# Sixteen of 22 pairs of column blocks of the upward feed-forward product as seven products of halves, on one Trainium2 core

## The chip, the core and the metric

The kernel runs on one core of a Trainium2 chip. A core has five engines that run side by side, each through its own queue in order: TensorE (PE) multiplies, VectorE (DVE) and ScalarE (ACT) work elementwise, GpSimd (POOL) does small things, and SyncE (SP) issues the transfers (DMA). PE writes into PSUM, eight banks of 128 x 512 f32; everything else lies in SBUF. The metric is the device time of one execution in microseconds; less is better.

## The reference

A trunk of two layers over 512 tokens of width 1024. Each layer has two feed-forward halves (FFN), a mixer of three head groups and a cross-attention. The change touches the FFN alone:

```python
def swiglu_ffn(x, w_up, w_down):
    gate, up = jnp.split(x @ w_up, 2, axis=-1)
    return (jax.nn.silu(gate) * up) @ w_down
...
    for i in range(DEPTH):
        g = norm_g[i]
        ff = swiglu_ffn(rms_norm(h, g[FFN1_PRE]), ffn_w_up[i, 0], ffn_w_down[i, 0])
        h = h + 0.5 * rms_norm(ff, g[FFN1_POST])
```

`w_up` is 1024 x 5632, `w_down` 2816 x 1024. The trunk has four FFNs. Everything is f32.

## The kernel before

**Products.** An f32 product is made of three matmuls of fp32r parts: every operand is split into hi (a rounded copy, made by ACT) and lo (the rest, a subtraction on DVE), and `mm3` (L243) issues hi x hi, hi x lo and lo x hi. `split` (L1317) is the pair of ACT and DVE operations.

**Upward.** The columns of `w_up` go in 44 blocks of 128, in pairs f = 0 to 21: one gate block, one up block. A block is one unit of weights, 1024 x 128, in SBUF as 128 x 1024: SP loads it into one of four raw buffers (`wraw`), `feed` (L436) splits it into `whi` and `wlo`, and `chans` (L637) multiplies it with the normalized, transposed input x (`xhi`, `xlo`, 1024 x 512 tokens) into one bank of PSUM (`ch`): 8 pieces of 128 rows x 3 matmuls, 512 columns each. The first four blocks of an FFN are made in two halves of 256 columns, because x comes token tile by token tile. `silu` (L853) takes silu of the gate bank (`sg`, ACT), multiplies it with the up bank (`hh`, DVE) and splits the result (`hid`, ACT and DVE).

**Downward.** `down` (L661) takes the 22 blocks of `hid` as the stationary operand and `w_down` as the moving one, 512 columns, for two token tiles of 128 at a time: two passes over 22 units of weights. The norm of the result, the update of h and the next x follow (`post`, `pre`).

**Order.** The program is written by generators ("streams": `feed`, `chans`, `silu`, `down` and so on). A planner in the kernel (`run`, L319) has a table of priorities (PRIO) and a rough clock for each engine, and writes down at each step the operation that could start first. What it writes is the order of each engine's queue; on the chip an engine takes its queue in order and waits on semaphores. In the first FFN three further streams run: `setup` with the rope tables, and `memory` (L869), which normalizes, transposes and splits the memory tokens (`mt`, `mn`, `mhi`, `mlo`).

Of the kernel before, what the change touches and what calls it, by code (L numbers as in the profile page):

```python
# [17 lines left out]
P = 128  # L18
# [37 lines left out]
def twice(order):  # L56
# [11 lines left out]
TAIL = 2, 3  # L68
WARM = 14
# [9 lines left out]
        "xhead": (30.98, 0.1), "square": (31.03, 0), "load": (32.65, 4), "none": (32.7, 0.5), "chans": (34.9, 0),  # L79
# [101 lines left out]
class Trunk:  # L181
# [34 lines left out]
    def raw(self, w, k0, nk, *cols):  # L216

        if len(cols) == 2 and isinstance(cols[0], int):
            cols = (cols,)
        n = sum(c[1] for c in cols)  # L220
# [38 lines left out]
class Weave:  # L259
# [3 lines left out]
    def __init__(self, trunk):  # L263
# [5 lines left out]
            "cur": CUR, "b": 8 - CUR, "w": 3, "raw": 4, "xn": 1, "y": 1, "sg": 1, "hh": 2, "jk": 1, "xq": 2, "xp": 2, "xpT": 2}.items()}  # L269
# [3 lines left out]
        self.u, self.raws = {}, {}  # L273
        self.made = self.used = 0
# [161 lines left out]
    def feed(self):  # L436

        k = self.k
        for i in range(len(self.todo)):
            yield ("r", i)  # L440
            raw = self.raws.pop(i)
            nk, n = raw.shape[1:]
            if i - NJ in self.first[1:]:

                yield ("x", self.first.index(i - NJ), NT - 1)
            o = APART if i in self.narrow else 0
# [3 lines left out]
            if i in self.extra:  # L450
                yield ("open", self.extra[i])
                if self.extra[i] == "x":
                    j = 2 * (len(self.todo) - 1 - i)
                    hi, lo = (flat(x[:, j:j + 2]) for x in (k.xhi, k.xlo))
# [5 lines left out]
            else:  # L460
                yield {"w": 1}
                hi, lo = (k.wp.tile([P, 1024 + 64], F32R, name=q, tag=q, bufs=3)[:, o:o + 1024] for q in ("whi", "wlo"))
# [5 lines left out]
            self.count(1, 0)  # L468

# [5 lines left out]
    def spent(self, i):  # L475
        del self.u[i]
        if i not in self.extra:
            self.free(w=1)
# [79 lines left out]
    def junk(self):  # L558
        mixer = self.phases[self.phase][1] == "mixer"
        key = "t2" if mixer else "jk"  # L560
        yield {key: 1}
        return key, self.t2("jk", [P, S]) if mixer else self.pool.tile([P, S], F32, name="jk", tag="jk")
# [74 lines left out]
    def chans(self, n, nj, sink):  # L637
# [15 lines left out]
        for i in range(nj, n):  # L653
            u = yield from self.unit(self.n(i))
# [6 lines left out]
    def down(self, x, i0, order, c, ready):  # L661
# [5 lines left out]
        for half in range(2):  # L667
# [11 lines left out]
            for i, q in enumerate(order):  # L679
                if half == 0 or i:  # L680
                    for e in ready(q, half):
                        yield e
# [8 lines left out]
                if half or i < nk - 1:  # L691
                    self.spent(self.n(n))
                    n += 1
            for t in ts:
                for f in range(2 if tail else 0):
                    cols = slice(f * S, (f + 1) * S)
                    for i, q, u, m in tail:
                        yield "T"
                        k.mm3x(ps[t][f:f + 1], x(q, t), [w[:, :, cols] for w in u], 0, i == 0, i == nk - 1)
                        if t == ts[1] and f:  # L700
                            self.spent(self.n(m))
                    if not f:
# [29 lines left out]
    def all(self):  # L732
# [5 lines left out]
        self.todo, self.first, self.extra, self.narrow = [], [], {}, set()  # L738
        self.mixers = [i for i, p in enumerate(self.phases) if p[1] == "mixer"]
        for i, p in enumerate(self.phases):  # L740
            self.first.append(len(self.todo))
            self.todo += self.units(*p)
            self.extra[self.first[i] + 3] = i
# [24 lines left out]
    def begin(self):  # L768
# [18 lines left out]
        for t in range(NT):  # L787
            xn = self.pool.tile([P, D], F32, name=f"xn{t}", tag=f"hid{NF - 11 - t}") if t else None
# [28 lines left out]
    def ffn(self, l, g):  # L817
        k = self.k
        wup = k.a["ffn_w_up"][l, g // 8]
        self.spare = (f"hid{NF - 8}", f"hid{NF - 9}")  # L820
        self.fired(("open", self.phase))
        self.hid = [None] * NF
# [7 lines left out]
        def sink(i, ps):  # L830
            if i % 2 == 0:
                self.gate = ps
            else:
                self.spawn(self.silu(i // 2, self.gate, ps), i)
            if i == 2 * NF - 1:
# [4 lines left out]
        def ready(q, half):  # L840
            return [] if half else [("hid", NF - 3 if q is None else q)]
# [3 lines left out]
        if self.phase == 0:  # L845
            self.spawn(self.memory())
        self.spawn(self.down(lambda q, t: tuple(self.hid[q][:, x, t * P:(t + 1) * P] for x in range(2)),
                             2 * NF, list(range(NF)), 0.5, ready))
# [4 lines left out]
    def silu(self, f, gate, up):  # L853
        yield {"sg": 1, "hh": 1}
        sg = self.pool.tile([P, S], F32, name="sg", tag="sg", bufs=1)
        hh = self.pool.tile([P, S], F32, name="hh", tag="hh", bufs=2)
# [1269 lines left out]
```

## Time and profile before

| | us |
|---|---|
| three runs: median (lowest, highest) | 2397.37 (2396.85, 2399.01) |
| the profiled execution, its own time | 2396.95 |
| its span, first to last instruction | 2395.2 |
| PE matmul, busy | 2369.4 |
| DVE, busy | 1306.8 |
| ACT, busy | 986.5 |

Busy time of PE is the union of the matmul records, which overlap: it tells that PE hardly ever stands still, not how fast it goes. How fast is read from starts: so many matmuls in so many microseconds. The same holds on a small scale for DVE, where a record is somewhat longer than the distance to the next start. PEld are the weight loads, one ahead of every matmul. The granted clock of PE was 1.00 in all the stretches shown.

### The profile page before, as it was taken

What the parts mean: (1) busy time and instruction counts of PE and PEld (TensorE: products, weight loads), DVE (VectorE), ACT (ScalarE), POOL (GpSimd) and SP (SyncE); (2) the same over time, 40 slices, a digit from 0 to 9 for tenths busy, and PEclk for the clock granted to TensorE, in tenths of its full rate; (3) what the DMA queues carried; (4) which work ended last, traced back from release to release, by engine and by line L of the source; (5) the groups of instructions that cost most, each with busy time, mean ns of one, the idle gap of its engine ahead of it and who ended that gap; (6) DMA issues with size and microseconds to landing.
All of it is one profiled execution on the core that took longest, in us unless ns stands there. A gap on an engine that the chain in (4) does not pass through costs nothing.

```text
span 2395.2 us, 31724 instructions
## 1 busy us (share of the span) xinstructions
PE 2369.4 (99%) x12398; PEld 2001.4 (84%) x12398; DVE 1306.8 (55%) x1926; ACT 986.5 (41%) x1627; POOL 285.7 (12%) x406
## 2 busy tenths in 40 slices
PE   9999999999999999999999999999999999999998
PEld 8888888878889888888888888897888898888887
DVE  5433456887766643334553334578876657333344
ACT  4332344534554542223442223445355545322343
POOL 1000001454200100000000000023442101000000
PEclk9999999999999999999999999999999999999999
DMA  6543455323555343335543334552145644333354
GB/s 177 160 132 97 151 198 145 93 59 118 176 203 176 123 124 97 97 97 177 179 129 97 97 97 172 195 127 84 60 131 180 210 151 140 107 97 97 98 194 157
DMA packets 320972, 323.23 MB, mean 135 GB/s; under 512 B 27075, under 2 KB 262069, under 8 KB 320822
## 3 DMA queue, kind: packets, MB, share of 16 engines
q1 hardware_dynamic: 320822, 321.20, 42.5%
q8 instruction: 97, 1.59, 0.3%
q14 instruction: 53, 0.43, 0.1%
HBM read 301.50 MB, written 19.66 MB: 134 GB/s over the span
## 4 chain that ended last, share of the span: by engine, by line
PE 92%; DVE 4%; ACT 1%; issue 1%; DMA 1%; POOL 1%; SPq 0%; DVEq 0%; POOLq 0%; ACTq 0%
PE ch L139 49%; PE dn L139 26%; PE kv L139 3%; PE tk L139 3%; PE tp L139 1%; PE xs L139 1%; PE xo L139 1%; PE mo L139 1%; PE ms L139 1%; PE iy L139 1%; PE iu L139 1%; PE kk L139 1%; PE mp L139 1%; DVE pair L139 1%; DVE p L139 1%
## 5 line engine op out<-in xcount | busy, mean ns | idle before, releaser
L139 ACT ACTIVATE whi<-wraw 128x1024 fp32r<-128x1024 f32 (+1 forms) x488 | 513.8, 1054 | 979.7 <-PE ch L139 603.2
L139 DVE TENSOR_TENSOR wlo<-wraw,whi 128x1024 fp32r<-128x1024 f32 (+2 forms) x487 | 594.3, 1221 | 579.6 <-ACT whi L139 565.1
L139 PE MATMUL ch<-xhi,whi 128*128 128x512 f32 (+1 forms) x1840 | 674.5, 369 | 0.0
L139 PE MATMUL ch<-xhi,wlo 128*128 128x512 f32 (+1 forms) x1840 | 669.8, 366 | 0.0
L139 PE MATMUL ch<-xlo,whi 128*128 128x512 f32 (+1 forms) x1840 | 657.7, 366 | 0.0
L139 PEld LDWEIGHTS ch<-xhi,wlo 128*128 128x128 f32 x1840 | 345.7, 188 | 57.5
L139 PEld LDWEIGHTS ch<-xhi,whi 128*128 128x128 f32 x1840 | 345.7, 188 | 57.3 <-issue 1.3
L139 PEld LDWEIGHTS ch<-xlo,whi 128*128 128x128 f32 x1840 | 339.1, 188 | 55.4
L139 PE MATMUL dn<-whi,hid 128*128 128x512 f32 x1376 | 373.6, 390 | 0.0
L139 PEld LDWEIGHTS dn<-whi,hid 128*128 128x128 f32 x1376 | 257.4, 188 | 53.0
L139 POOL TENSOR_SCALAR ss<-ss 128x1 f32<-128x1 f32 (+1 forms) x80 | 32.6, 408 | 1656.0 <-ACT jk L139 1512.5
L139 PE MATMUL dn<-wlo,hid 128*128 128x512 f32 x688 | 214.0, 389 | 0.0
L139 DVE TENSOR_TENSOR hh<-sg,ch 128x512 f32<-128x512 f32 x88 | 60.5, 687 | 261.0 <-PE ch L139 257.0
L139 PEld LDWEIGHTS dn<-wlo,hid 128*128 128x128 f32 x688 | 129.1, 188 | 26.9
L139 PE MATMUL tk<-whi,xhi 128*128 128x272 f32 (+2 forms) x192 | 71.7, 374 | 0.0
L139 PE MATMUL tk<-whi,xlo 128*128 128x272 f32 (+2 forms) x192 | 67.4, 351 | 0.0
L139 PE MATMUL tk<-wlo,xhi 128*128 128x272 f32 (+2 forms) x192 | 67.1, 350 | 0.0
L139 POOL TENSOR_TENSOR sr<-tri,hl 128x512 fp32r<-128x512 f32 x48 | 56.7, 1190 | 65.0 <-PE sg L139 39.5
L139 PE MATMUL dn<-whi,xhi 128*128 128x512 f32 x192 | 61.8, 396 | 0.0
L139 DVE TENSOR_TENSOR hid<-hh,hid 128x512 fp32r<-128x512 f32 x88 | 60.2, 684 | 2.4 <-ACT hid L139 2.4
L139 ACT ACTIVATE xhi<-tp 128x512 fp32r<-128x512 f32 x64 | 37.4, 593 | 58.5 <-PE tp L139 58.2
L139 PE MATMUL dn<-wlo,xhi 128*128 128x512 f32 x192 | 60.9, 391 | 0.3 <-DVE wlo L139 0.2
(338 smaller groups left out, 2887.0 us busy)
## 6 DMA issues: line engine op xcount, KB each, us to landing
wraw<-in_ffn_w_up_dram SPq DMA_DIRECT2D x176, 512.0 KB
wraw<-in_ffn_w_down_dram SPq DMA_DIRECT2D x172, 512.0 KB
wraw<-in_w_in_dram SPq DMA_DIRECT2D x32, 512.0 KB
wraw<-in_xa_w_kv_dram SPq DMA_DIRECT2D x32, 512.0 KB
wraw<-in_w_out_dram SPq DMA_DIRECT2D x30, 512.0 KB
wraw<-in_xa_w_o_dram SPq DMA_DIRECT2D x30, 512.0 KB
mch<-memT SPq DMA_DIRECT2D x32, 256.0 KB
xkv<-kvs SPq DMA_DIRECT2D x32, 256.0 KB
```

Of the source, the lines that this page charges most:

```text
L139: return f(*args, **kw)
```

## The change

In each FFN 16 of the 22 pairs (f = 3 to 20 without 9 and 15) are computed otherwise. A pair is a product of 2 x 2 block matrices: the weights by gate/up and by the halves of the 1024 rows (512 each), x by the same halves of rows and by the halves of the tokens (256 each). Eight products of halves give the result; the change takes seven (Strassen's scheme in Winograd's form), of sums of halves.

- `units` and `raw` load a pair as two buffers X and Y of two half-blocks each, every half with a DMA of its own.
- `feed7` makes four pieces: a (X as it is), c and b (sums, in the tile `sums`: three DVE operations of 1024, 512 and 512 elements) and d (half of Y). a, b and c have 1024 elements in a row, d has 512. Each is split as before. There is one more place for weights in an FFN (four, and two halves for d).
- `forms` makes four sums of quarters of x (`form`), once in an FFN, and splits them.
- `products` issues seven products of 4 pieces x 3 matmuls with 256 columns, into four banks; in the order of PE: P1 (a), P6 (c), P2 (d), P7 (c), P5 (b), P3 (b), P4 (a). The banks are called p17, p62, p5 and p34 (the order rows print p).
- `combine` adds them up: a copy on ACT, four operations on DVE (tile `w`), then silu on ACT and the product with it on DVE (`hid`, now kept in f32).
- `hsplit` splits the results of all 22 pairs in the downward product, for each of its two passes the half of the tokens that the pass needs (`hs`); the places for it are those of the sums of x. The split in `silu` goes.
- `memory` starts when the sums of x are there and uses other buffers; a few tiles move; the scratch of the software DMA, which the kernel does not use, is made smaller. The table of priorities gets a line for each of the new streams.

```diff
+SEVEN = [f for f in range(3, NF - 1) if f not in (9, 15)]
...
-        "xhead": (30.98, 0.1), "square": (31.03, 0), "load": (32.65, 4), "none": (32.7, 0.5), "chans": (34.9, 0),
+        "xhead": (30.98, 0.1), "square": (31.03, 0), "load": (32.65, 4), "forms": (33.5, 0), "piece": (31.5, 0.1), "combine": (2.9, 0), "hsplit": (30.5, 0), "split": (33.4, 0), "none": (32.7, 0.5), "chans": (34.9, 0),
...
+    def feed7(self, i):
+        X, Y = (flat(self.raws.pop(j)).rearrange("p (i n) -> p i n", i=2) for j in (i, i + 1))
+        V = self.V
+        yield {"w": 1}
+        a = self.spawn(self.piece((i, "a"), tuple(self.slot((i, "a"), APART)), X))
+        t = self.pool.tile([P, 4, 512], F32, name="sums", tag="sums")
+        yield "V"
+        V.tensor_tensor(out=t[:, 0:2], in0=bc(Y[:, 1], 1, 2), in1=X, op=ALU.add)
+        yield "V"
+        V.tensor_tensor(out=t[:, 2], in0=t[:, 0], in1=X[:, 1], op=ALU.add)
+        yield {"w": 1}
+        c = self.spawn(self.piece((i, "c"), tuple(self.slot((i, "c"), APART)), t[:, 1:3]))
+        yield "V"
+        V.tensor_tensor(out=t[:, 3], in0=t[:, 2], in1=Y[:, 0], op=ALU.add)
+        yield {"w": 1}
+        b = self.spawn(self.piece((i, "b"), tuple(self.slot((i, "b"), APART)), t[:, 0:4:3]))
+        yield {"wh": 1}
+        h = self.halves
+        self.halves = 1 - h
+        d = self.spawn(self.piece((i, "d"), tuple(self.pool.tile([P, 512 + 64], F32R, name=q, tag=f"{q}h{h}")[:, APART:APART + 512] for q in ("whi", "wlo")),
+                                  Y[:, 0:1]))
+        yield a
+        self.free(raw=1)
+        yield d
+        self.free(raw=1)
+        yield c
+        yield b
...
+            if self.n(i) in self.seven:
+                yield from self.products(i)
+            if self.n(i) in self.seven or self.n(i - 1) in self.seven:
+                continue
...
+    def products(self, i):
+        f, i = i // 2, self.n(i)
+        yield ("forms",)
...
+        a = yield from self.unit((i, "a"))
+        yield {"cur": 1}
+        ps = bank("p17")
+        self.spawn(self.combine(f, banks), 2 * f)
+        yield from prod(ps[:, lo], a, 0, x(0, 0))
+        self.fire(("P1", f))
+        c = yield from self.unit((i, "c"))
+        yield {"cur": 1}
+        p2 = bank("p62")
+        yield from prod(p2[:, lo], c, 1, s2)
+        d = yield from self.unit((i, "d"))
+        yield from prod(p2[:, hi], d, 0, x(1, 0))
+        self.fire(("P2", f))
+        self.spent((i, "d"))
+        yield from prod(ps[:, hi], c, 0, s3)
+        self.fire(("P7", f))
+        self.spent((i, "c"))
+        b = yield from self.unit((i, "b"))
+        yield {"cur": 1}
+        yield from prod(bank("p5")[:, lo], b, 0, s1)
+        self.fire(("p5", f))
+        yield {"cur": 1}
+        ps = bank("p34")
+        yield from prod(ps[:, hi], b, 1, x(1, 1))
+        self.spent((i, "b"))
+        yield from prod(ps[:, lo], a, 1, s4)
+        self.fire(("p4", f))
+        self.spent((i, "a"))
...
+    def combine(self, f, banks):
...
+        w = self.pool.tile([P, 6, 256], F32, name="w", tag="w")
+        yield ("P1", f)
+        yield "S"
+        SC.activation(out=w[:, 4], in_=banks["p17"][:, 0:256], func=AF.Copy)
+        yield ("P2", f)
+        yield "V"
+        V.tensor_tensor(out=w[:, 0:6:5], in0=two(banks["p62"]), in1=bc(w[:, 4], 1, 2), op=add)
+        self.drop(banks["p62"])
+        yield ("P7", f)
+        yield "V"
+        V.tensor_tensor(out=w[:, 1], in0=banks["p17"][:, 256:512], in1=w[:, 0], op=add)
+        self.drop(banks["p17"])
+        yield ("p5", f)
+        yield "V"
+        V.tensor_tensor(out=w[:, 0:4:2], in0=bc(banks["p5"][:, 0:256], 1, 2), in1=w[:, 0:2], op=sub)
+        self.drop(banks["p5"])
+        yield ("p4", f)
+        yield "V"
+        V.tensor_tensor(out=w[:, 3:5], in0=two(banks["p34"]), in1=w[:, 0:2], op=add)
+        self.drop(banks["p34"])
+        yield {"sg": 1}
+        sg = self.pool.tile([P, 2, 256], F32, name="sg", tag="sg", bufs=1)
+        yield "S"
+        SC.activation(out=sg, in_=w[:, 4:6], func=AF.Silu)
+        yield "V"
+        V.tensor_tensor(out=two(self.hidden(f)), in0=w[:, 2:4], in1=sg, op=ALU.mult)
+        self.free(sg=1, seven=1)
+        self.swapped.add(f)
+        self.fire(("hid", f))
...
+    def forms(self):
...
+        a11, a12, a21, a22 = f32
+        self.sx = [form(j) for j in range(4)]
+        t11, t21, t = temp(10), temp(9), temp(8)
+        yield from add(t11, *a11)
+        yield from add(t21, *a21)
+        yield from add(t, t11, t21, ALU.subtract)
+        last = [self.spawn(self.split(*self.sx[2], t))]
+        yield from add(t21, t21, a22[0], ALU.subtract)
+        yield from add(t21, t21, a22[1], ALU.subtract)
+        last.append(self.spawn(self.split(*self.sx[0], t21)))
+        yield from add(t11, t21, t11, ALU.subtract)
+        last.append(self.spawn(self.split(*self.sx[1], t11)))
+        yield last[0]
+        yield from add(t, t11, a12[0])
+        yield from add(t, t, a12[1])
+        last.append(self.spawn(self.split(*self.sx[3], t)))
+        for e in last:
+            yield e
+        self.fire(("forms",))
...
+    def hsplit(self):
+        for half in range(2):
+            order = list(range(NF))[::1 - 2 * half]
+            for q in order:
+                yield ("hid", q)
+                h = 1 - half if q in self.swapped else half
+                yield {"hs": 1}
+                j = self.hs_free.pop(0)
+                t = self.pool.tile([P, 4, 256], F32R, name="hs", tag=f"form{j}")[:, 0:2]
+                yield from self.split(t[:, 0], t[:, 1], self.hid[q // 2][:, q % 2, 256 * h:256 * h + 256])
+                self.hs[q, half] = t, j
+                self.fire(("hs", q, half))
...
-            up = [(a["ffn_w_up"][l, j], 0, KD, s * FF + f * P, P) for f in range(NF) for s in range(2)]
+            w, up = a["ffn_w_up"][l, j], []
+            for f in range(NF):
+                c0, c1 = f * P, FF + f * P
+                if f in SEVEN:
+                    up += [(w, 0, KD, [(0, c0), (4, c1)]), (w, 0, KD, [(4, c0), (0, c1)])]
+                else:
+                    up += [(w, 0, KD, c, P) for c in (c0, c1)]
             return up + [(a["ffn_w_down"][l, j], q, 1, 0, D) for q in twice(range(NF))]
...
         def ready(q, half):
-            return [] if half else [("hid", NF - 3 if q is None else q)]
+            return [("hs", q, half)] if q is not None else [] if half else [("hid", NF - 3)]
...
         yield "V"
-        self.V.tensor_tensor(out=hh, in0=sg, in1=up, op=ALU.mult)
+        self.V.tensor_tensor(out=self.hidden(f), in0=sg, in1=up, op=ALU.mult)
...
-        t = self.hid[f] = self.pool.tile([P, 2, S], F32R, name=f"hid{f}")
-        yield from self.split(t[:, 0], t[:, 1], hh)
-        self.free(hh=1)
...
-        yield ("hid", 3)
+        yield ("forms",)
+        yield {"xn": 1, "y": 1}
```

The order of DVE before, in the upward stretch of the second FFN; `hh` and `hid` are one pair's product with silu and its split, `wlo` splits of blocks:

```order
L139 TENSOR_TENSOR hh<-sg,ch 128x512 [waits PE_49,Activation_49]
L139 TENSOR_TENSOR wlo<-wraw,whi 128x1024 [waits DMAHW7_49,Activation_49]
L139 TENSOR_TENSOR hid_11694<-hh,hid_11694 128x512 [waits Activation_49]
L139 TENSOR_TENSOR wlo<-wraw,whi 128x1024 [waits DMAHW0_49,PE_49,Activation_49]
L139 TENSOR_TENSOR hh<-sg,ch 128x512 [waits PE_49,Activation_49]
L139 TENSOR_TENSOR wlo<-wraw,whi 128x1024 [waits DMAHW1_49,Activation_49]
L139 TENSOR_TENSOR hid_11767<-hh,hid_11767 128x512 [waits Activation_49]
```

The order of DVE after, in the same stretch, one changed pair; `w<-p` are the combinations of pair f (in turn p62, p17, p5, p34), `sums` and `wlo` the feed of pair f+1 (splits of a, c, b, d in turn), `hid` the product with silu of pair f:

```order
L141 TENSOR_TENSOR sums<-wraw 128x1024 [waits DMAHW6_49,DMAHW4_49,DMAHW3_49]
L141 TENSOR_TENSOR w<-p_12698,w 128x2x256 [waits PE_49,Activation_49]
L141 TENSOR_TENSOR wlo<-wraw,whi 128x1024
L141 TENSOR_TENSOR w<-p_12683,w 128x256 [waits DVE_49,PE_49]
L141 TENSOR_TENSOR sums<-sums,wraw 128x512
L141 TENSOR_TENSOR w<-p_12751,w 128x2x256 [waits DVE_49,PE_49]
L141 TENSOR_TENSOR sums<-sums,wraw 128x512 [waits DMAHW5_49,DVE_49]
L141 TENSOR_TENSOR wlo<-sums,whi 128x1024 [waits Activation_49]
L141 TENSOR_TENSOR w<-p_12765,w 128x512 [waits DVE_49,PE_49]
L141 TENSOR_TENSOR wlo<-sums,whi 128x1024 [waits Activation_49]
L141 TENSOR_TENSOR hid_12836<-w,sg 128x512 [waits Activation_49]
L141 TENSOR_TENSOR wlo<-wraw,whi 128x512
```

Twelve operations stand where four stood, and the split of d comes last, behind the product with silu. In every second pair of a block of changed pairs the last two stand the other way round.

The order of PE before, at the start of a block of 512 columns in the same FFN:

```order
L139 MATMUL ch<-xhi,whi 128x512 [waits Activation_49]
L139 MATMUL ch<-xlo,whi 128x512
L139 MATMUL ch<-xhi,wlo 128x512 [waits DVE_49]
L139 MATMUL ch<-xhi,whi 128x512
L139 MATMUL ch<-xlo,whi 128x512
```

The order of PE after, in the pair that follows the DVE rows above, at the step from P6 (sums of x, weights c) to P2 (x itself, weights d); both write the bank p62:

```order
L141 MATMUL p_12820<-form,whi 128x256 x2
L141 MATMUL p_12820<-form,wlo 128x256
L141 MATMUL p_12820<-xhi,whi 128x256 [waits Activation_49]
L141 MATMUL p_12820<-xlo,whi 128x256
L141 MATMUL p_12820<-xhi,wlo 128x256 [waits DVE_49]
L141 MATMUL p_12820<-xhi,whi 128x256
```

As before, the third matmul of a piece waits for DVE's `wlo`; it now waits for the split of d, the last of the twelve.

The order of DVE before, in the first FFN, where the memory tokens are split:

```order
L139 TENSOR_TENSOR wlo<-wraw,whi 128x1024 [waits DMAHW1_49,PE_49,Activation_49]
L139 TENSOR_TENSOR mn<-mt_759,mg_875 128x1024 [waits DMAHW4_49]
L139 TENSOR_TENSOR mlo<-mp,mhi 128x512 [waits Activation_49]
L139 TENSOR_TENSOR hh<-sg,ch 128x512 [waits PE_49,Activation_49]
L139 TENSOR_TENSOR wlo<-wraw,whi 128x1024 [waits DMAHW2_49,Activation_49]
L139 TENSOR_TENSOR hid_978<-hh,hid_978 128x512 [waits Activation_49]
```

The order of DVE after, in the first FFN, in the feed of its third changed pair (`xn<-mt` is what was `mn`):

```order
L141 TENSOR_TENSOR w<-p_891,w 128x2x256 [waits DVE_49,PE_49]
L141 TENSOR_TENSOR wlo<-sums,whi 128x1024 [waits Activation_49]
L141 TENSOR_TENSOR w<-p_906,w 128x512 [waits DVE_49,PE_49]
L141 TENSOR_TENSOR xn<-mt_628,y 128x1024 [waits DMAHW6_49]
L141 TENSOR_TENSOR hid_988<-w,sg 128x512 [waits Activation_49]
L141 TENSOR_TENSOR wlo<-sums,whi 128x1024
L141 TENSOR_TENSOR wlo<-wraw,whi 128x512
L141 TENSOR_TENSOR mlo<-mp,mhi 128x512 [waits Activation_49]
```

The operations on the memory tokens stand between the combinations and the splits b and d of the next pair; rope operations stand between those of the two pairs ahead.

## Rows read from the trace of the kernel before

**Rows 1.** The page: span; instructions by engine; the chain's shares
```profile
span 2395.2 us, 31724 instructions
...
PE 2369.4 (99%) x12398; PEld 2001.4 (84%) x12398; DVE 1306.8 (55%) x1926; ACT 986.5 (41%) x1627; POOL 285.7 (12%) x406
...
PE 92%; DVE 4%; ACT 1%; issue 1%; DMA 1%; POOL 1%; SPq 0%; DVEq 0%; POOLq 0%; ACTq 0%
PE ch L139 49%; PE dn L139 26%; PE kv L139 3%; PE tk L139 3%; PE tp L139 1%; PE xs L139 1%; PE xo L139 1%; PE mo L139 1%; PE ms L139 1%; PE iy L139 1%; PE iu L139 1%; PE kk L139 1%; PE mp L139 1%; DVE pair L139 1%; DVE p L139 1%
```
**Rows 2.** Chain in five stretches: start us, us, matmuls; first four 256 columns, last 512
```profile
26.08 12.03 PE ch L139 x102
...
852.93 11.07 PE ch L139 x94
...
1217.88 10.22 PE ch L139 x90
...
2039.48 10.60 PE ch L139 x90
...
902.83 57.35 PE ch L139 x253
```
**Rows 3.** Windows: busy us of each engine, clock, DMA share, GB/s
```profile
900.00:1000.00 100.00, 100.00 (x443) 82.81 (x442) 33.98 (x37) 28.79 (x36) 0.00 (x0) 1.00 0.33 98
105.00:135.00 30.00, 30.00 (x141) 24.79 (x140) 15.71 (x18) 11.03 (x17) 0.00 (x0) 1.00 0.71 206
960.00:970.00 10.00, 10.00 (x46) 8.27 (x45) 3.23 (x4) 3.20 (x4) 0.00 (x0) 1.00 0.36 105
853.00:863.00 10.00, 10.00 (x87) 10.00 (x86) 5.03 (x6) 5.93 (x8) 0.00 (x0) 1.00 0.50 174
```
**Rows 4.** Timeline of PE where an FFN's first block begins: start us, record us, instruction
```profile
1203.77 0.39 PE L139 MATMUL dn<-whi,hid 128*128 128x512 f32 x1
1203.99 0.28 PE L139 MATMUL ch<-xhi,whi 128*128 128x256 f32 x1
1204.11 0.28 PE L139 MATMUL ch<-xhi,wlo 128*128 128x256 f32 x1
1204.23 0.28 PE L139 MATMUL ch<-xhi,whi 128*128 128x256 f32 x1
```
**Rows 5.** Timeline of DVE in one pair of blocks; in brackets the wait before
```profile
963.00 0.69 DVE L139 TENSOR_TENSOR hh<-sg,ch 128x512 f32<-128x512 f32 x1 [3.37 <-PE ch L139]
963.80 1.23 DVE L139 TENSOR_TENSOR wlo<-wraw,whi 128x1024 fp32r<-128x1024 f32 x1
964.94 0.68 DVE L139 TENSOR_TENSOR hid<-hh,hid 128x512 fp32r<-128x512 f32 x1
969.28 1.23 DVE L139 TENSOR_TENSOR wlo<-wraw,whi 128x1024 fp32r<-128x1024 f32 x1 [3.66 <-ACT whi L139]
```
**Rows 6.** Timeline of DVE: operations back to back that read PSUM
```profile
479.40 1.28 DVE L139 TENSOR_TENSOR xdt<-px,spp 128x512 f32<-128x512 f32 x2
480.59 0.68 DVE L139 TENSOR_TENSOR y<-px,b_ssd_d 128x512 f32<-128x512 f32 x1
...
489.61 0.42 DVE L139 TENSOR_TENSOR Am<-kk,E 128x256 f32<-128x256 f32 x1 [0.87 <-PE kk L139]
489.95 0.41 DVE L139 TENSOR_TENSOR QK<-kk,E 128x256 f32<-128x256 f32 x1
```
**Rows 7.** Timelines of PE and ACT in the same pair
```profile
962.73 0.39 PE L139 MATMUL ch<-xhi,whi 128*128 128x512 f32 x1
...
962.70 1.06 ACT L139 ACTIVATE whi<-wraw 128x1024 fp32r<-128x1024 f32 x1 [3.84 <-PE ch L139]
963.72 0.63 ACT L139 ACTIVATE hid<-hh 128x512 fp32r<-128x512 f32 x1
```
**Rows 8.** Groups of DVE instructions by form, first FFN, 45 to 165 us
```profile
L139 DVE TENSOR_TENSOR mlo<-mp,mhi 128x512 fp32r<-128x512 f32 x8 | 5.5, 690 | 8.2 <-ACT mhi L139 5.3 <-DMA memT<-mlo 2.9
L139 DVE TENSOR_TENSOR mn<-mt,mg 128x1024 f32<-128x1024 f32 x4 | 4.9, 1215 | 0.0
L139 DVE SCALAR_TENSOR_TENSOR rope<-rope 128x64 f32<-128x64 f32 x8 | 1.8, 224 | 0.2
L139 DVE TENSOR_SCALAR mt<-mt,mss 128x1024 f32<-128x1024 f32 x2 | 1.5, 753 | 1.5 <-POOL mss L139 1.5
```
**Rows 9.** Waits of SyncE's queue, 900 to 1040 us: total us, times, longest
```profile
SPq L225 <- DVE wlo L139: 129.8, 26, 5.1
```

More of the change, by code (lines that the diff above doesn't have):

```diff
@@ L273, in __init__ @@
         self.u, self.raws = {}, {}
+        self.slots, self.slot_of, self.own = [(0.0, i) for i in range(3)], {}, False
         self.made = self.used = 0
@@ L476, in spent @@
         del self.u[i]
-        if i not in self.extra:
-            self.free(w=1)
+        s = self.slot_of.pop(i, None)
+        if s is None:
+            if isinstance(i, tuple):
+                self.free(wh=1)
+        elif s < 3 or self.own:
+            self.back(s)
     def count(self, made, used):
@@ L659, in chans, with x, prod, bank @@
             sink(i, ps)
-    def down(self, x, i0, order, c, ready):
+    def products(self, i):
+        k = self.k
+        f, i = i // 2, self.n(i)
+        yield ("forms",)
+        def x(kh, th):
+            return tuple(q[:, 4 * kh:4 * kh + 4, 256 * th:256 * th + 256] for q in (k.xhi, k.xlo))
+        def prod(out, u, h, x, first=True, last=True):
+            for kk in range(4):
+                if kk % 2 == 0:
+                    yield "T"
+                k.mm3(out, tuple(q[:, 4 * h:4 * h + 4] for q in u), kk, (x[0][:, kk], x[1][:, kk]), first and kk == 0, last and kk == 3)
+        lo, hi = slice(0, 256), slice(256, 512)
+        s1, s2, s3, s4 = self.sx
+        def bank(name):
+            ps = self.bank(name, True)
+            banks[name] = ps
+            return ps
+        banks = {}
+        a = yield from self.unit((i, "a"))
[26 more added lines that the diff above has]
+        self.spent((i, "a"))
@@ new lines, in hidden @@
+    def hidden(self, f):
+        assert self.phase or f < 14 or self.event(("memory",)).t is not None
+        if f % 2 == 0:
+            self.hid[f // 2] = self.pool.tile([P, 2, S], F32, name=f"hid{f // 2}")
+        return self.hid[f // 2][:, f % 2]
+    def hsplit(self):
[10 more added lines that the diff above has]
+                self.fire(("hs", q, half))
@@ L663, in down @@
+    def down(self, x, i0, order, c, ready, done=None):
         k = self.k
@@ L679, in down @@
             for i, q in enumerate(order):
+                for e in ready(q, half):
+                    yield e
                 if half == 0 or i:
-                    for e in ready(q, half):
-                        yield e
                     u = yield from self.unit(self.n(n))
@@ L693, in down @@
                     n += 1
+                if done is not None:
+                    done(q, half)
             for t in ts:
@@ L701, in down @@
                             self.spent(self.n(m))
+                            if done is not None:
+                                done(q, half)
                     if not f:
@@ L1258, in rope @@
         k, V, S_ = self.k, self.V, self.S
[L1259 removed]
+        room = self.pool.tile([P, D], F32, name="rope", tag="hid6")
         def part(n):
```

114 lines of the change are left out of this document (94 added, 20 removed).

## The prediction, made before the changed kernel ran

> **What bounds the kernel now.** The page comes first: TensorE (PE) has 2369.4 us of matmul in a span of 2395.2 us, and the chain that ended last is PE for 92%, the column-block products alone (tile ch) for 49% [rows 1]. So a matmul that goes away in the upward stretches shortens the run, as long as nothing becomes late in its place. Next comes the pace of that chain: 253 matmuls of 512 columns take 57.35 us, 0.2267 us each [rows 2]. The records themselves (0.39 us) overlap, so pace is read from starts and counts. VectorE (DVE) splits the weights and is 34% busy in an upward stretch [rows 3]. It waits, 3.4 to 3.7 us at a time, for PE or for ScalarE (ACT), which itself waits for PE [rows 5]. That idle time is what the change spends, so DVE is the second thing to read.
>
> **What the change removes and adds on PE.** An ordinary pair is 2 x 8 x 3 = 48 matmuls of 512 columns: 48 x 0.2267 = 10.88 us. A changed pair is 7 products x 4 x 3 = 84 matmuls of 256 columns. Such matmuls run today in the first four blocks of each FFN: 0.1179, 0.1178, 0.1136 and 0.1178 us each in four stretches [rows 2]. In them the weight loads fill 10.00 of 10.00 us, against 8.27 at 512 columns [rows 3]: a load is issued for every matmul, so half the columns is not quite half the time. Entering from a 512-column stream, as the changed pairs do, the pace starts at 0.12 [rows 4]; I take the mean of the four, 43.92 us / 376 = 0.1168. A changed pair is then 9.81 us and saves 1.07 us; 16 pairs x 4 FFNs = 64 pairs save **68.5 us**. The ends: 0.1136 gives 85.7 us, 0.1179 gives 62.4 us.
>
> By the Trainium skill, page "TensorE: Matmul & The Clock Gate", section "Back-to-back issue gap", starts are N/2.4 + 2.5 ns apart, 215.8 and 109.2 ns here, and the saving would be 76 us. The rows show both widths slower than that, so the measured paces stand.
>
> **What it adds on DVE, in the steady pair.** Spacing counts, not the record: a 1024-element op takes 1.14 us to the next start (963.80 to 964.94, record 1.23) [rows 5]; two 512-element ops that read PSUM take 1.19 us, 0.60 each, and a 256-element one 0.34 [rows 6]. Per changed pair DVE has four ops of 1024 (one sum, the splits of a, b, c), seven of 512 (two sums, the split of d, three combinations, the product with silu) and one of 256: 4.56 + 4.20 + 0.34 = **9.10 us** of 9.81. It fits with 0.7 us over, where today it has 2 x 1.14 + 2 x 0.60 = 3.5 of 10.88. ACT gets three copies of 1024 at 1.06, two ops of 512 of at most 0.63 [rows 7] and one of 256: at most 5.1 of 9.81, no bound.
>
> **Who waits for whom.** DVE takes its queue in order, and the order rows show the feed of pair f+1 woven with the combination of pair f. I set them beside PE's order: P1 (weights a), P6 (c), P2 (d), P7 (c), P5 (b), P3 (b), P4 (a), 1.40 us each. From the first matmul of the next block to the DVE op that reads the finished bank it is 0.27 us (962.73 to 963.00) [rows 5, 7]. Pieces a, b and c are ready over 1.5 us before their product. Piece d is not, where its split stands behind the product with silu (the first order fence of after): 0.27 + 0.60 (p34) + 1.14 (split b) + 0.60 (silu product) + 0.69 (record of split d) = 3.30 us after P4 ends. PE wants wlo of d for the third matmul of P2, 2 x 12 + 2 = 26 matmuls or 3.04 us after. With the load ahead of that matmul the gap is about 0.4 us. It comes 6 times in each of the three later FFNs and 4 times in the first: 22 x 0.4 = **9 us** lost. Bounds: 0, if PE loads lie later than I think; 15 us at 0.7 each. Where the split of d stands ahead, it is done over 0.5 us early.
>
> **The first FFN.** There DVE also normalizes and splits the memory tokens: 8 splits (mlo) and 4 multiplications of 1024 (mn), two of mt, and the rope operations [rows 8]. Before, they lay in DVE's waits. Now they start after the sums of x and lie in the first block of six changed pairs (the second order pair): 8 x 0.60 + 4 x 1.14 + 2 x 0.67 + some 15 small ones at 0.2 = 13.7 us, against 5 x 0.7 = 3.5 us of slack. PE waits for weights for about **10 us**. Bounds: 5 us, if the ordinary pair that follows and the weights made ahead take up more; 14 us, if they take up none.
>
> **The sums of x.** Eight additions of 1024 and four splits run on DVE in each FFN, after the last piece of x is there. With weights and products of the first pairs between, DVE has done piece c of the first changed pair after 16 ops of 1024 and 4 of 512 by the order, 16 x 1.14 + 4 x 0.60 = 20.6 us. PE until then has the second halves of four blocks (96 matmuls at 0.1168, 11.2 us), two blocks of 512 (10.9 us) and P1 (1.4 us): 23.5 us. It is covered with 2.9 us over, less what DVE waits for ACT in between; with that cover gone it would be some 2 us in each FFN. I put 0.5 us each, **2 us** (0 to 8).
>
> **At nothing.** The four banks of a pair come free by the combination long before the next pair asks for the same one. The split of the results moves to the downward product: 44 more DVE ops of 0.34 in an FFN, one to a step of 12 x 0.2267 = 2.72 us in which DVE has 1.14 of weights; uncovered, it would be 0.3 us per step. SyncE issues two DMAs of half the size for a changed block; the same bytes come a little faster, 98 x 10.88/9.81 = 109 GB/s, and another stretch of the same FFNs moves 206 [rows 3]; today its queue waits for buffers, not for data [rows 9].
>
> **Sum.** 68.5 - 9 - 10 - 2 = 47.5 us. The profiled execution took 2396.95 us (span 2395.2); that gives 2349.5, and against the median of 2397.37 us **2350 us**, taken as 2349.
>
> **Rivals.**
> 1. DVE is the bound. If an op started only where the record of the one before ends (1.23 and 0.69 [rows 5], 0.42 [rows 6]), a pair would take 4 x 1.23 + 7 x 0.69 + 0.42 = 10.17 us of DVE: 0.71 us saved, 45 us in all, less 10 for the first FFN with 5 more for its fuller queue: 2397 - 30 = **2367 us**. The trace speaks against it (964.94 comes before 963.80 + 1.23), but at 34% busy it never shows twelve such ops in a row that wait for three engines, and an op that needs the one just ahead of it does wait out its record. Chance 0.2. The Trainium skill states it in "VectorE: DVE Perf Modes", section "The DRAIN you can't avoid": the next op does not start until the pipe is empty. By that rule this rival would be the forecast; the spacings of the rows are shorter than it allows.
> 2. The fast pace. After some interruptions the 256-column stream runs at 0.1136 [rows 2]. Were that the pace throughout: 85.7 - 21 = 65 us, **2332 us**. Chance 0.15.
> 3. Slower than before. DVE's in-order queue opens at each of the four places where it reads a PE result, because PE stalls and DVE then waits for PE in turn: full records (10.17) and 4 x 0.27 us of exposed hand-over make 11.25 us a pair. From 10.88 us on, that is 1.78 us of waiting on top of 9.10, the change loses; at 11.25 it loses 64 x 0.37 = 24 us, and 10 in the first FFN: **2431 us**. Against it: only the first of the four comes where DVE has run ahead of PE. Chance 0.05.
> That the change does not do what it says is no rival: the order has 3072 matmuls of 512 columns fewer and 5376 of 256 more, which is 64 x 48 and 64 x 84.
>
> **How the numbers follow.** Forecast 0.6, rivals 0.2, 0.15 and 0.05. The forecast's own range is 2334 to 2369: its unknowns (pace up to 0.1179, and the bounds of the three losses) reach from -16 to +22 if all fall one way. The range that should hold 8 in 10 reaches over the first rival and most of the second: 2328 to 2373. A measurement of this kernel can tell about 0.2%, 4.8 us, from no change. Forecast and both first rivals lie below that, with a small part of the first above: faster 0.93, same 0.03, slower 0.04.
>
> **What would show it.** In the profile after, 84 matmuls of 256 columns at 0.113 to 0.118 in a changed pair, so a pair every 9.8 us in the three later FFNs, and every second one with a wait of PE for wlo of 0.3 to 0.5 us (step on d). DVE at over 90% there. In the first FFN, between the sums of x and the tenth pair, PE waits for DVE of 10 us. No PE wait in the downward product. If pairs come every 10.2 us or more in all four FFNs with DVE's ops a record apart, rival 1 holds. What makes it wrong: a pace of 256-column matmuls over 0.12 with the new operands, which no row shows.

## The result, and the profile after

The changed kernel takes **2339.4 us** (median of 4 runs, 2338.4 to 2341.7) against 2397.2 for the kernel before beside it (4 runs, 2396.9 to 2399.0): the ratio is 0.9759, with a 95% interval of 0.9742 to 0.9776. The forecast was 2349, its own range 2334 to 2369. The gain is 57.8 us where 47.5 were predicted.

From the page of the kernel after, the lines that answer to [rows 1]:

```profile
span 2336.9 us, 37944 instructions
...
PE 2302.3 (99%) x14702; PEld 2045.0 (88%) x14702; DVE 1764.3 (75%) x2638; ACT 1130.0 (48%) x1923; POOL 290.0 (12%) x406
...
PE 88%; DVE 8%; ACT 1%; issue 1%; POOL 1%; DMA 1%; SPq 0%; DVEq 0%; POOLq 0%; ACTq 0%
PE dn L141 27%; PE p L141 23%; PE ch L141 19%; PE kv L141 3%; PE tk L141 3%; DVE wlo L141 2%; PE tp L141 1%; PE xs L141 1%; PE xo L141 1%; PE mo L141 1%; PE ms L141 1%; DVE w L141 1%; DVE hid L141 1%; PE iy L141 1%; PE iu L141 1%
```

PE still sets the end, but DVE now holds 8% of the chain (4% before), with three operations named: the splits (wlo), the combination (w) and the product with silu (hid). The chain of one stretch of five changed pairs shows where they stand in it (start us, us, engine, tile, line, count; two short pieces are left out):

```profile
929.99 6.34 PE ch L141 x28
936.33 19.80 PE p L141 x168
956.13 0.02 issue
956.16 0.69 DVE w L141
956.85 0.80 DVE wlo L141
...
957.90 0.68 DVE hid L141
958.58 0.61 DVE wlo L141
959.20 0.04 issue
959.24 16.39 PE p L141 x142
...
975.66 0.69 DVE w L141
976.35 0.80 DVE wlo L141
...
977.40 0.68 DVE hid L141
978.08 0.61 DVE wlo L141
978.70 0.04 issue
978.74 6.87 PE p L141 x58
985.61 10.90 PE ch L141 x48
```

This is the wait for piece d, in the order that the prediction named: combination, split of b, product with silu, split of d. Windows of the same stretch (columns as in [rows 3]): the whole, two pairs before the first wait, and most of a pair behind it; the last one is the first downward product.

```profile
900.00:1000.00 100.00, 99.60 (x768) 95.21 (x767) 83.59 (x105) 41.98 (x54) 0.00 (x0) 1.00 0.38 111
936.30:955.90 19.60, 19.60 (x169) 19.60 (x168) 15.40 (x20) 8.03 (x11) 0.00 (x0) 1.00 0.27 79
966.10:975.40 9.30, 9.30 (x85) 9.30 (x84) 9.03 (x12) 4.13 (x7) 0.00 (x0) 1.00 0.31 91
...
250.70:372.30 121.60, 121.60 (x545) 100.47 (x544) 76.38 (x100) 64.29 (x106) 6.34 (x10) 1.00 0.63 186
```

DVE is busy for 83.59 of 100 us where it was 33.98, and the weights come at 111 GB/s (109 predicted). The downward product has no gap in PE, so the 44 splits moved there are hidden.

One thing in these rows was not in the prediction. By the starts of the matmuls, the first two pairs of this stretch take 9.89 us each, 0.1178 us a matmul; the pair after the first wait takes 9.52, 0.1133 us. The instructions are the same, and the granted clock is 1.00 in both windows, so the clock does not make the difference. Both paces stand in [rows 2] (0.1178 and 0.1136), but I averaged them. Over all 5376 matmuls, waits apart, the mean is 0.1150 us.

By starts, PE waits 17.6 us in the changed pairs: 8.6 in the first stretch of the first FFN, and 9.0 in the others. Of these 9.0, 8.7 are the 22 waits for d, of 0.33 us at the slower pace and 0.44 at the quicker.

### The profile page after: what moved, and what is told of

It reads as the page before. It is cut to its first block, busy times and chain, and to the rows that moved or that the text cites. A ratio compares the mean times of both kernels' runs of the same rounds, so it can differ in the third digit from the quotient of the medians.

```text
span 2336.9 us, 37944 instructions
## 1 busy us (share of the span) xinstructions
PE 2302.3 (99%) x14702; PEld 2045.0 (88%) x14702; DVE 1764.3 (75%) x2638; ACT 1130.0 (48%) x1923; POOL 290.0 (12%) x406
## 4 chain that ended last, share of the span: by engine, by line
PE 88%; DVE 8%; ACT 1%; issue 1%; POOL 1%; DMA 1%; SPq 0%; DVEq 0%; POOLq 0%; ACTq 0%
PE dn L141 27%; PE p L141 23%; PE ch L141 19%; PE kv L141 3%; PE tk L141 3%; DVE wlo L141 2%; PE tp L141 1%; PE xs L141 1%; PE xo L141 1%; PE mo L141 1%; PE ms L141 1%; DVE w L141 1%; DVE hid L141 1%; PE iy L141 1%; PE iu L141 1%
## 5 line engine op out<-in xcount | busy, mean ns | idle before, releaser
L141 ACT ACTIVATE whi<-wraw 128x1024 fp32r<-128x1024 f32 (+2 forms) x492 | 488.3, 993 | 385.6 <-PE dn L141 185.3
L141 PE MATMUL dn<-whi,hs 128*128 128x512 f32 x1376 | 373.5, 390 | 0.0
L141 PE MATMUL p<-form,whi 128*128 128x256 f32 x2048 | 362.3, 278 | 0.0
L141 PEld LDWEIGHTS p<-form,whi 128*128 128x128 f32 x2048 | 310.9, 188 | 0.0
L141 PEld LDWEIGHTS dn<-whi,hs 128*128 128x128 f32 x1376 | 257.4, 188 | 52.9
L141 PE MATMUL ch<-xhi,whi 128*128 128x512 f32 (+1 forms) x880 | 293.3, 338 | 0.0
L141 PE MATMUL ch<-xhi,wlo 128*128 128x512 f32 (+1 forms) x880 | 289.4, 334 | 0.8 <-DVE wlo L141 0.6
L141 PE MATMUL p<-form,wlo 128*128 128x256 f32 x1024 | 284.5, 278 | 0.4 <-DVE wlo L141 0.4
L141 PE MATMUL ch<-xlo,whi 128*128 128x512 f32 (+1 forms) x880 | 277.2, 334 | 0.0
L141 PE MATMUL p<-xhi,wlo 128*128 128x256 f32 x768 | 216.6, 282 | 7.2 <-DVE wlo L141 6.6
```

Source lines behind the costliest of these rows:

```text
L141: return f(*args, **kw)
```

## The experiments

Three questions: what sets the pace, how full DVE is, and what the first FFN's waits come from. "The changed kernel" is 2339.4 us throughout. Stretch means an unbroken run of changed pairs, 3 in each FFN.

### Taking the wait for d away

**d ahead of b.** In `feed7` the two lines that make piece b move down behind the lines of piece d:

```
         V.tensor_tensor(out=t[:, 3], in0=t[:, 2], in1=Y[:, 0], op=ALU.add)
-        yield {"w": 1}
-        b = self.spawn(self.piece((i, "b"), tuple(self.slot((i, "b"), APART)), t[:, 0:4:3]))
         yield {"wh": 1}
...
                                   Y[:, 0:1]))
+        yield {"w": 1}
+        b = self.spawn(self.piece((i, "b"), tuple(self.slot((i, "b"), APART)), t[:, 0:4:3]))
         yield a
```

> The split of piece d is queued ahead of the split of piece b, so that PE should no longer wait for d (about 9 us of waits in the changed kernel). Theory A (a wait of PE for weights is what turns the pace of the 256-column products from 0.118 to 0.113 us): the waits go, and with them the faster pace behind them, about 13 us in 42 pairs, partly kept where another wait stands at the start of a stretch: 2338 to 2344 us, with pairs of 9.89 us to the end of each stretch. Theory B (the pace has nothing to do with the wait, it goes by the place in the stretch): pairs of 9.52 us from the fourth of a stretch on as now, 9 us gained, 2330 us.

Measured: **2351.1 us** (ratio to before 0.9809, 0.9794 to 0.9823), outside what either theory gave. The chain in one stretch:

```profile
943.46 44.53 PE p L141 x378
987.99 0.02 issue
988.01 0.39 ACT w L141
988.40 0.04 issue
988.45 5.05 PE p L141 x42
```

378 matmuls in a row without a wait for d, at 0.1178 us. So far theory A. The mean pace in the changed pairs is now 0.1167 instead of 0.1150, 5376 x 0.0016 = 8.8 us lost, and the time over it says that waits did not shrink: 20.1 us instead of 17.6. Each of the eleven later stretches has a new one of 0.75 us in its fifth pair, the one shown. ACT's timeline there (in brackets the wait before):

```profile
988.01 0.38 ACT L141 ACTIVATE w<-p 128x256 f32<-128x256 f32 x1 [2.58 <-PE p L141]
```

That is ACT's copy of P1. It waits for PE until six matmuls of P7 are done, which go to the other half of the same bank, and PE's seventh waits for the copy. The rows read as if the planner, with d's operations earlier, had issued the copy in the middle of P7, so that the two take turns on one bank; this was not tried by itself. The waits of the first FFN's first stretch also grew, from 8.6 to 11.1 us, and two spells of 3.4 us at a granted clock of 0.50 in it cost another 2.6.

**The product with silu behind d.** This reaches the same end without putting anything else off: in `combine` the last DVE operation becomes a stream of its own with a low rank, so that DVE splits d first.

```
-        yield "V"
-        V.tensor_tensor(out=two(self.hidden(f)), in0=w[:, 2:4], in1=sg, op=ALU.mult)
...
+            self.spawn(self.gated(f, w, sg))
+
+    def gated(self, f, w, sg):
+        yield "V"
+        self.V.tensor_tensor(out=self.hidden(f).rearrange("p (i n) -> p i n", i=2), in0=w[:, 2:4], in1=sg, op=ALU.mult)
```

> The changed kernel with its 16 pairs, and in every changed pair the product with silu queued behind the split of d. The 22 waits for d go (9 us). Theory A2: with them goes what turned the pace to the fast one, so that stretches which begin slow stay slow, 9.89 us a pair to their end: 9 us gained and as much lost, 2337 to 2342 us. If the pace has nothing to do with the waits: 2330 us.

Measured: **2341.5 us** (0.9766, 0.9751 to 0.9781), as theory A2 had it. The chain in the stretch shown above is now one piece of five whole pairs, 0.1178 us a matmul from end to end:

```profile
934.88 3.17 PE ch L141 x14
938.06 49.47 PE p L141 x420
987.52 2.52 PE ch L141 x11
```

All waits for d are gone, 9 us. The mean pace rose to 0.1168, 5376 x 0.0018 = 9.7 us. The waits for d had bought back what they cost. Position is ruled out: the last pairs of a stretch run at either pace. Of the eleven later stretches only two ran at 0.1133, those with a wait of 0.15 us in their first pair; one of them fell back to 0.1178 in its last pair, after a halt of 0.06 us.

### Making a wait on purpose

**With a small matmul.** On d ahead of b, in the first changed pair of each stretch:

```
         self.fire(("P1", f))
+        if i - 2 not in self.seven:
+            pin = self.pool.tile([P, P], F32R, name="pin", tag="pin")
+            yield "S"
+            self.S.activation(out=pin, in_=ps[:, 0:P], func=AF.Copy)
+            yield "T"
+            self.T.matmul(ps[:, 256:320], pin, x(0, 0)[0][:, 0, :64], start=True, stop=True)
```

> As the run with d ahead of b, and in the first changed pair of each stretch one more small matmul (64 columns, its output is overwritten) whose weights are a copy by ACT of the bank that PE has just finished: PE must wait for weights once, some 0.7 us, 12 times in all. Theory A: from there on every pair of the stretch at 0.113 us a matmul, 9.52 us a pair: 15 us faster than the run with d ahead of b, 2323 to 2329 us. Theory B: nothing gained behind the wait, 8 us slower than the run with d ahead of b.

Measured: **2364.7 us** (0.9867, 0.9851 to 0.9884), outside both, and 13.6 us slower than without. PE lost 0.9 us at each of the 12 places and in most stretches went on at 0.1178 until the next wait. The quicker pace followed at once only in two, which had it from the second pair on in the first experiment too. So theory A as first stated, that any wait for weights turns the pace, falls.

**Without one.** On d ahead of b, in the first pair of a stretch DVE reads a column of P6 before it splits d, so that PE waits for d itself:

```
+            yield ("P6", gate)
+            yield "V"
+            self.V.tensor_copy(self.pool.tile([P, 1], F32, name="pin", tag="pin"), self.p6[:, 0:1])
+            yield "V"
+            self.V.tensor_tensor(out=lo, in0=src, in1=hi.bitcast(F32), op=ALU.subtract)
```

> As the run with d ahead of b, but in the first changed pair of each stretch DVE splits d only after it has read one column of P6, so PE waits for d between two 256-column matmuls, with no small matmul in between. Theory A2 (any interruption draws the pace of the stream anew, and a wait between two 256-column matmuls mostly draws the fast one: 47 of 52 such waits in the runs so far; the 64-column matmul behind the wait of the last try drew the slow one): 9.52 us a pair from the second pair on in at least 9 of 12 stretches, some 18 us gained on the run with d ahead of b, less 12 waits of 0.9 us: 2340 to 2346 us. Theory B (the place in the stretch decides): 9.89 us a pair as before, 2360 us or more.

Measured: **2363.8 us** (0.9861, 0.9843 to 0.9878): wrong on the time, and 7 stretches of 12 turned instead of 9. The chain:

```profile
950.23 0.17 DVE pin L141
950.40 0.14 issue
950.54 0.47 PE p L141 x2
951.04 21.25 PE p L141 x184
972.30 0.02 issue
972.32 0.39 ACT w L141
```

After the wait made on purpose the matmuls are 21.25 / 184 = 0.1155 us apart, the rest of the waits among them, and the next pair takes 9.61 us. The mean pace is 0.1149. But the wait of P7 for ACT's copy now comes in two pairs of every later stretch (0.74 us, at either pace), and the waits sum to 39.6 us: the step that failed is that I took the other waits of this order as given.

Taken together, without the run with the small matmul: in the traces of twelve kernels I compared the pace in the dozen matmuls before and after each wait inside a stretch. Of 112 waits that came at 0.1178, 94 left 0.1133 behind; of 155 that came at 0.1133, 12 left 0.1178. So each wait draws the pace anew, mostly the quicker one. Many of these waits stand at the same place of the same order, so they are not so many independent draws. Entering a stretch from 512 columns without a wait always drew 0.1178. Between waits the pace stays. In the eleven later stretches of all thirteen changed kernels 4751 dozens of matmuls have no wait in them: 2864 run at the quicker pace, 1868 at the slower, none in between, and 19 at 0.120. All 19 stand in P2 of the run just shown, and only in that run does the pace change without a wait. Why is open: I found nothing in the records ahead of a wait that tells how it goes, and waits of 0.34 us at the same place went either way.

### Does the quicker pace last?

**All 18 pairs.** `SEVEN = [f for f in range(3, NF - 1)]`, without the exclusion of 9 and 15.

> All 18 pairs from the fourth to the last but one by products of halves, with no ordinary pair in between: 8 more changed pairs, and two entries from 512-column matmuls fewer in each FFN. Theory A: 8 x (10.88 - 9.74) = 9 us for the pairs and 8 entries x 1 us because the pace is not lost at the tenth and the sixteenth pair: 2322 us. Theory B: 8 x 1.05 = 8 us, 2331 us. Theory C (DVE has no time left over in a changed pair, and the ordinary pairs let it catch up): the waits of PE grow from pair to pair, and nothing is gained, 2339 us or more.

Measured: **2328.5 us** (0.9715, 0.9700 to 0.9729), 10.9 below the changed kernel and between theories A and B. The pace gained (0.1139) but the waits for d, now in every second pair to the end, grew, and with them all waits, from 17.6 to 23.1 us. Theory C falls: the waits stay at 0.44 us through 18 pairs.

**d ahead of b from the fifth pair.** The 18 pairs with the move of the first experiment in the later FFNs:

> All 18 pairs changed, and in the three later FFNs, from the fifth changed pair on, the split of d is queued ahead of that of b: the first pairs still have their wait for d, the later ones have none. Theory A2: the fast pace, once drawn, lasts without further waits: the run with 18 pairs less 3 x 7 waits of 0.44 us, plus a wait of 0.75 us for b at each end: 2320 to 2323 us. If the fast pace needs a wait every two pairs to last: 14 pairs x 3 at 9.89 us instead of 9.74: 2334 us.

Measured: **2340.0 us** (0.9760, 0.9745 to 0.9776), a miss for both. The wait for d is gone, and in its place, in every second pair, stands one of 0.80 us for the lower half of another piece, at the end of a chain that begins with ACT's late copy of P1. Waits sum to 30.1 us. The question had to be put by another order.

**The product with silu behind d from the fourth pair:**

> All 18 pairs changed, and from the fourth changed pair on the product with silu is queued behind the split of d instead of ahead of it; nothing else is moved, so b is not put off as it was when d was queued ahead of it. That brings d 0.60 us sooner, more than the 0.44 us that PE waits for it. Theory A2 (the fast pace, once drawn by the first waits, lasts): the run with 18 pairs less some 27 waits of 0.44 us: 2315 to 2320 us. If the fast pace does not last without waits: 9.89 us a pair instead of 9.75, 2332 us or more. If another piece is late next, as b was: 2325 us or more.

Measured: **2320.6 us** (0.9679, 0.9663 to 0.9695), at the edge of what A2 gave. Two pieces of its chain, the second FFN and the first:

```profile
904.89 130.11 PE p L141 x1148
...
129.92 115.19 PE p L141 x978
```

In the second FFN 130.11 / 1148 = 0.1133 us, more than 13 pairs without any wait: the quicker pace lasts by itself. In the first FFN 115.19 / 978 = 0.1178 us: the last waits of its sixth pair, with 3.4 us at a granted clock of 0.50 behind them, had left the slower one, and it lasted as well. Both paces hold until something interrupts them.

**The same, later in the first FFN** (from its seventh pair):

> As the last run with 18 pairs, but in the first FFN the product with silu stays ahead of the split of d until the ninth product block of halves or so, as in the changed kernel, so that the waits there leave the stream in the fast pace; in the last run they left it in the slow one for 12 pairs. Theory A2: the first FFN gains 12 x 0.37 = 4.4 us on the last run and the waits of the fast pace stay away: 2313 to 2318 us. If the waits of the first FFN happen to leave the slow pace again: 2320 us.

Measured: **2316.5 us**, median of 5 runs (0.9666, 0.9651 to 0.9680), the lowest median here, though not clear of the run before it: the intervals overlap. In the profiled run the first FFN drew 0.1178 again at its seventh pair, so the gain hoped for there is not shown. The five runs spread over 8.6 us, from 2312.4 to 2321.0, twice what 12 pairs at either pace are worth (12 x 0.37 = 4.4 us). Only one of them has a trace, so what spread them stays open.

### How full is DVE?

One 1024-element sum of each changed pair made twice:

```
         V.tensor_tensor(out=t[:, 0:2], in0=bc(Y[:, 1], 1, 2), in1=X, op=ALU.add)
+        yield "V"
+        V.tensor_tensor(out=t[:, 0:2], in0=bc(Y[:, 1], 1, 2), in1=X, op=ALU.add)
```

> One more DVE operation of 1024 elements in each changed pair (the first sum is made twice, the result is the same). By the spacings of the prediction DVE then needs 9.10 + 1.14 = 10.24 us a pair, against pairs of 9.74 us in the mean in the changed kernel: DVE becomes the bound, pairs come every 10.2 us once what was made ahead is used up, 64 x 0.5 = 32 us less about 1 us made ahead in each of 12 stretches, 2355 to 2371 us. Rival 1 of the prediction (an operation starts only where the record before it ends): 10.17 + 1.23 = 11.4 us a pair, 2440 us. If DVE has more room than counted: 2339 to 2345 us.

Measured: **2383.1 us** (0.9942, 0.9926 to 0.9958). A window of two steady pairs:

```profile
911.00:931.60 20.60, 19.62 (x171) 19.23 (x170) 20.60 (x27) 9.24 (x13) 0.00 (x0) 1.00 0.35 102
```

DVE (third number) is busy for all of it. A pair comes every 10.29 us by the starts, also where PE runs at 0.1178, so DVE is the bound. Less the 1.14 us added, a pair needs 9.15 of DVE; the prediction counted 9.10. Rival 1's 11.4 us is out. The total went 12 us over the range because I had left out the first FFN, whose first stretch, already overfull, went from 8.6 to 17.5 us of waits and lost some 5 more at a granted clock of 0.50.

### The first FFN

Waits of PE and the DVE window there, kernel after:

```profile
PE p L141 <- DVE wlo L141: 4.8, 5, 1.9
PE mp L141 <- DVE xn L141: 1.0, 1, 1.0
...
55.00:122.00 67.00, 60.95 (x509) 59.05 (x508) 64.32 (x101) 31.62 (x47) 1.82 (x3) 1.00 0.60 172
```

(This view counts from the end of a matmul's record, so it shows less than the starts do.)

**DVE's work on the memory tokens left out.** A first try, with 2331 to 2334 us expected, stored the one upper half twice from one buffer. ACT then waited 10.4 us for the transfers out of it, with DVE behind: 2342.0 us, which tells nothing of the cause. The second:

> As the last try to leave out DVE's work on the memory tokens (two scalings, four multiplications, eight lower halves; the upper half is stored twice), but with two buffers in turn for the upper half, since in that try ACT waited 10 us for the transfers out of the one buffer, with DVE and PE behind it. As predicted: at most 1 us of PE waits in the first stretch of six pairs, 6 to 8 us gained on the changed kernel, 2331 to 2334 us (up to 2 us more if the slow pace lasts longer without waits). Rival (transposes, banks or the rope operations make the waits): 2337 us or more.

Measured: **2333.2 us** (0.9732, 0.9717 to 0.9746), 6.3 below the changed kernel; by the starts 1.5 us of waits are left in the stretch, of 8.6. In the view of waits:

```profile
PE p L141 <- DVE wlo L141: 0.5, 1, 0.5
```

DVE's work is the cause. The prediction's step stands.

**The same work moved to GpSimd.** The scalings go likewise; shown are the multiplications:

```
-                yield "V"
-                V.tensor_tensor(out=mn, in0=mt[i], in1=g, op=ALU.mult)
+                yield "G"
+                self.G.tensor_tensor(out=mn, in0=mt[i], in1=g, op=ALU.mult)
```

> In the first FFN the two scalings of the memory tokens and their four multiplications by the gain go from DVE to GpSimd, 4 x 1.14 + 2 x 0.67 = 5.9 us less on DVE in the first stretch of six changed pairs. If the 8 us that PE waits there are DVE's work on the memory tokens, as predicted: 1 to 3 us of waits are left, and 4 to 6 us are gained (2334 to 2336), less up to 1.9 us under theory A, which takes the faster pace away from pairs with no wait ahead of them. If they come from something else (the transposes on PE, the banks, the copies on ACT): no change, 2339 us.

Measured: **2338.4 us** (0.9755, 0.9741 to 0.9770), no change that can be told from none. The waits of the first stretch fell only from 8.6 to 7.1 us, and the mean pace in the changed pairs was 0.1154, which costs 2 us. The window shown above for the changed kernel has DVE as busy as before, with six operations of 1024 fewer:

```profile
55.00:122.00 67.00, 62.33 (x513) 60.43 (x512) 64.74 (x94) 31.07 (x46) 19.47 (x10) 1.00 0.55 160
```

Timelines of DVE and of GpSimd (start, record, instruction):

```profile
64.64 2.06 DVE L141 TENSOR_TENSOR sums<-wraw 128x1024 f32<-128x1024 f32 x1
...
67.89 2.42 DVE L141 SCALAR_TENSOR_TENSOR rope<-rope 128x64 f32<-128x64 f32 x1
70.23 0.68 DVE L141 TENSOR_TENSOR w<-p,w 128x512 f32<-128x512 f32 x1
...
64.38 2.98 POOL L141 TENSOR_SCALAR mt<-mt,mss 128x1024 f32<-128x1024 f32 x1
67.33 2.90 POOL L141 TENSOR_TENSOR xn<-mt,y 128x1024 f32<-128x1024 f32 x1
```

An operation of 64 elements that takes 0.22 us elsewhere takes 2.42 and ends within 0.1 us of GpSimd's (67.33 + 2.90 = 70.23); a sum of 1.22 us takes 2.06. Both read two operands from SBUF. In the whole window the sums of 512 elements took 0.99 us each instead of 0.68. What was taken off DVE came back as blocked time. The Trainium skill says so in "SBUF — State Buffer", section "Who interferes with whom": a VectorE instruction with two SBUF inputs contends with a GpSimd instruction that reads SBUF, and issue order decides which one waits. The trace agrees for the operation of 64 elements, which started behind GpSimd's.

## Why the prediction was right, step by step

- **What bounds the kernel: right.** PE's matmuls in the upward stretches, and next DVE's order.
- **Matmuls removed: right mechanism, term mis-sized.** 0.1168 us was the mean of the stretches in [rows 2]; 0.1150 was measured. 64 pairs x 84 x 0.0018 = 9.7 us, nearly all of the 10.3 us by which the gain was underestimated. The step that was off is "I take the mean of the four": the four held two discrete paces, and the question was which one each stretch would get. The 215.8 and 109.2 ns set beside it from the Trainium skill, "TensorE: Matmul & The Clock Gate", section "Back-to-back issue gap", are given there for an isolated matmul; both paces here are slower than 109.2. The waits that the prediction charged as pure loss also drew the quicker one. The second rival was half there, and the run at 2320.6 us shows its pace over 13 pairs in a row.
- **DVE in the steady pair: right.** 9.10 us counted, 9.15 measured with DVE made the bound. The spacings of [rows 5, 6] recur in the timeline after, starts 1.13, 0.61, 0.59 and 0.34 us apart:

```profile
960.24 1.22 DVE L141 TENSOR_TENSOR wlo<-wraw,whi 128x1024 fp32r<-128x1024 f32 x1
961.37 0.68 DVE L141 TENSOR_TENSOR w<-p,w 128x512 f32<-128x512 f32 x1
961.98 0.68 DVE L141 TENSOR_TENSOR sums<-sums,wraw 128x512 f32<-128x512 f32 x1
962.57 0.41 DVE L141 TENSOR_TENSOR w<-p,w 128x256 f32<-128x256 f32 x1
962.91 0.68 DVE L141 TENSOR_TENSOR sums<-sums,wraw 128x512 f32<-128x512 f32 x1
```

  So rival 1 falls by its own figure. Its rule from the Trainium skill, "VectorE: DVE Perf Modes", section "The DRAIN you can't avoid", was only half read: the section goes on that a next operation which is not held starts earlier, and the starts above agree with that.
- **The wait for d: right,** 9 us predicted and 8.7 measured in 22 waits, in the chain of DVE operations that was named. The difference between its two sizes, 0.11 us, is what 26 matmuls gain at the quicker pace (26 x 0.0045 = 0.12).
- **The first FFN: right, a little oversized,** 10 predicted, 8.6 measured, within 5 to 14. Leaving the work out took 7.1 of it away.
- **The sums of x: right, oversized.** 2 us predicted; only waits of 0.15 us stand in the first pairs of the second and fourth FFN.
- **At nothing: right.** The first downward product takes 121.6 us, 121.4 before; about 3 us of the whole difference are left, in places I did not follow.
- **Rival 3: not seen.** It needed 1.78 us of waiting a pair; 0.22 were there in the steady pairs. The longest DVE queue, with an operation more in each pair, still stayed below the time before.

## What to carry to other kernels

Where rows show two values for the pace of one instruction stream, look for two states and for what sets them, before taking a mean. An engine filled from 34% to 84% brings waits that come from the order of its queue rather than from its load; moving the one operation that nobody needs soon behind the one that somebody waits for was worth 8 us with 18 changed pairs, where it was done from the fourth pair on and the quicker pace had been drawn. With 16 pairs, done in every pair, it gained nothing, because the slower pace stayed. Moving the awaited operation up cost 12 us: it put off something else, and most of the cost was again the pace. Moving work to an idle engine helps only if the two don't block each other.

## What the runs showed of the hardware

- Streams of 256-column fp32r matmuls, each with its own weight load, run at 0.1133 or at 0.1178 us a matmul, and keep the one they are in, for 1148 and 978 matmuls in a row without change. Why a wait draws one or the other stays open.
- GpSimd at work on SBUF blocked VectorE operations with two SBUF operands: 0.22 us became 2.42.
- With d ahead of b, two waits of 1.1 and 1.2 us that ended 1.5 us apart were followed by 3.4 us at half clock, granted 0.50, the lower of the two levels, 1.2 GHz; a single wait of 2.0 us in the kernel after was not:

```profile
74.90:76.40 1.50, 1.50 (x9) 1.50 (x9) 1.50 (x3) 0.53 (x3) 0.00 (x0) 0.50 0.00 0
```
